# Out-state weights of an S5 layer on three engines: power 0 to ScalarE, input products to VectorE, one-input forms for the smallest VectorE operations

## The chip, the core and the metric

The kernel runs on one core of a Trainium2 chip as one program. The metric is device time in microseconds. Five engines run their own in-order instruction queues and wait for one another through semaphores: TensorE (PE, matmul), VectorE (DVE), ScalarE (ACT), GpSimd (POOL) and SyncE (SP), which here issues nearly all DMAs.

## The reference

Two post-norm layers share one residual stream of 512 latent and 256 context tokens, 1024 wide. Layer 0 is windowed grouped-query attention, layer 1 a bidirectional diagonal state space (S5). Cut to what matters:

```python
for i in range(2):
    h = x * (1 + scale) + shift; hc = xc * (1 + scale_c) + shift_c
    pz = h @ w_in; pzc = hc @ w_in          # p: mixer input, z: gate path
    y, yc = attention_mixer(...) if i == 0 else s5_mixer(...)
    x = layer_norm(alpha * x + gate * ((y * silu(z)) @ w_out), g, b)
    if i == 0:                              # the same for xc
        xc = layer_norm(alpha * xc + gate_c * ((yc * silu(zc)) @ w_out), g, b)

def softmax_with_sink(s, sink):             # one more logit per head
    return softmax(concat([s, sink]))[..., :-1]

def s5_scan(u, abar, bbar, cmat, h0):       # per 128-token chunk, 2 directions
    bu = einsum('btgn,gpn->btgp', u, bbar)  # complex states, 64 per group
    hs = associative_scan(a * h + bu)
    y = einsum('btgp,gnp->btgn', hs, cmat).real
```

abar, bbar and cmat depend on parameters alone. The kernel computes from them, while layer 0 runs, the weights with which layer 1 works on blocks of tokens.

## The kernel before

**The weights.** Layer 1 needs 64 in-state weights (`gen_w`) and 32 out-state weights (`gen_o`, numbered q = 0 to 31). One out-state weight is two halves `gO` of 128 x 576: 4 groups by 9 powers (0 to 8) of the transition by 16 channels. Each half is a real and an imaginary product and their sum: L931 (`gO` = `gcb` x powers), L932 (`gX`, the same with the other part), L933 (`gO` = `gO` + `gX`). Before them three small operations make the input coefficients: L919 and L920 (two products of 128 x 128, into the two halves of a `gX` tile) and L921 (`gbb`, 128 x 256, their sum). All run on POOL, except for q = 3, 7 and 11, which run on DVE as a whole. `gX` has one buffer for both engines, `gO` four (three in the second pool), `gcb`, `gpp` and `gbb` two each.

**What follows a weight.** SP writes the halves to DRAM (`osc`, L936). A closure `lag` then multiplies `gbb` with `gO` on PE (L948, 16 short matmuls), ACT and DVE copy the result to `gK` (L954 to L957), and SP writes it to `ksc` (L958); every eighth weight also starts eight DMAs that reorder it (`m0sc`, L974). The lag of one weight is issued behind the products of the next. PE works through its queue in order, so a lag whose weight is late holds up all matmuls behind it.

**Where the weights are made.** Layer 0 calls `bg(n)` between its steps; behind the in-state weights it opens a pool `go` (`open_o`, four `gO` buffers) and asks for out-state weights 0 to QA - 1 = 26. The output projection of layer 0 (`outproj0`) calls `side()` between token blocks; the first NB = 3 calls make the other five from a pool `go2` with three `gO` buffers. A scheduler with priorities sets each engine's order; a weight's products are given a priority of GP = 80 ahead of their place, a lag LP = 50.

**Attention.** `att_s` takes two heads at a time: scores on PE (`S`), mask and negated maximum on DVE (L445, L453, and L454 on context tokens, 128 x 2), exponentials on ACT (L461, L463), the row sum plus sink (L464, 128 x 2) and its reciprocal on DVE, the scaling on ACT (L467). `att_o` transposes on PE (`PT`), splits into a high and a low half on ACT and DVE (`pth`, `ptl`) and multiplies with the values.

**The norm and layer 1's input.** `norm` takes statistics on DVE and an inverse root by an integer guess and three Newton steps of two operations each on 128 x 1 (L293, L294); `nrm` (L631) normalizes 128 x 512. `make_h1` transposes the rows on PE (`h1t`), applies scale and shift on 128 x 128 pieces, four on DVE (L1018) and four on ACT (L1020) of each eight, and splits the result into `H1H` (ACT) and `H1L` (DVE). In `outproj0` PE multiplies the gated attention (`gr`, split to `gh` and `gl`) with `wout` (split to `woh` and `wol`) into `po`.

Every fp32 matmul operand goes through such a split and every product is three matmuls (L155 to L157).

## Time and profile before

| | us |
|---|---|
| median of 3 runs (1504.64 to 1512.83) | 1510.47 |
| the profiled execution | 1508.56 |
| its span in the trace | 1506.8 |
| PE busy | 1404.2 (93%) |
| DVE busy | 1040.2 (69%) |
| ACT busy | 645.8 (43%) |
| POOL busy | 635.0 (42%) |

The mean granted clock of PE was 0.971 of full speed. Each engine's busy time is the sum over its instructions; the share is of the span. An engine that is busy for less than the span was either not needed or waiting, and which of the two it was is read stage by stage. Stages in the trace: layer 0 up to about 655 us (the last in-state weight leaves POOL at 468.25 us and out-state weights follow), `outproj0` from there to about 870 us, then layer 1.

### The profile page before, as it was taken

What the parts mean: (1) busy time and instruction counts of PE and PEld (TensorE: products, weight loads), DVE (VectorE), ACT (ScalarE), POOL (GpSimd) and SP (SyncE); (2) the same over time, 40 slices, a digit from 0 to 9 for tenths busy, and PEclk for the clock granted to TensorE, in tenths of its full rate; (3) what the DMA queues carried; (4) which work ended last, traced back from release to release, by engine and by line L of the source; (5) the groups of instructions that cost most, each with busy time, mean ns of one, the idle gap of its engine ahead of it and who ended that gap; (6) DMA issues with size and microseconds to landing.
All of it is one profiled execution on the core that took longest, in us unless ns stands there. A gap on an engine that the chain in (4) does not pass through costs nothing.

```text
span 1506.8 us, 25662 instructions
## 1 busy us (share of the span) xinstructions
PE 1404.2 (93%) x9092; PEld 1134.5 (75%) x9092; DVE 1040.2 (69%) x2711; ACT 645.8 (43%) x1256; POOL 635.0 (42%) x542
## 2 busy tenths in 40 slices
PE   7999999999997899987988799999999999999997
PEld 2554789988886788875766688888777777888886
DVE  7734748777684477876759922789887896565376
ACT  1310546555464446552333234445556545343220
POOL 0004469999998676988975800000000000000240
PEclk9999999999998899998999899999999999999999
DMA  9876566766664446488795476667666796655541
GB/s 335 274 232 203 163 192 202 225 214 208 200 221 152 131 146 200 141 248 265 214 280 158 137 257 226 210 210 231 220 226 220 223 292 213 197 195 168 180 152 60
DMA packets 252639, 309.57 MB, mean 205 GB/s; under 512 B 45408, under 2 KB 151648, under 8 KB 252512
## 3 DMA queue, kind: packets, MB, share of 16 engines
q1 hardware_dynamic: 227168, 295.36, 61.5%
q10 hardware_dynamic: 25344, 12.59, 2.9%
q8 instruction: 71, 1.16, 0.3%
q14 instruction: 56, 0.46, 0.1%
HBM read 239.20 MB, written 77.07 MB: 210 GB/s over the span
## 4 chain that ended last, share of the span: by engine, by line
PE 54%; POOL 13%; DVE 13%; DMA 10%; issue 5%; ACT 3%; SPq 1%; POOLq 0%; DVEq 0%; ACTq 0%
PE pg L155 4%; PE pg L157 4%; PE pg L156 4%; PE adaps L166 3%; PE po L156 3%; PE po L157 3%; PE po L155 3%; DMA wsc<-gW 3%; PE ins L1084 3%; POOL gm L885 3%; POOL gm L886 2%; PE pul L155 2%; PE pul L156 2%; PE pul L157 2%; POOL gW L888 2%
## 5 line engine op out<-in xcount | busy, mean ns | idle before, releaser
L1318 POOL TENSOR_TENSOR xt<-xt,lng 128x512 f32<-128x512 f32 (+1 forms) x9 | 13.7, 1532 | 584.5 <-DMA xt<-n0sc 584.5
L146 DVE TENSOR_TENSOR wl<-wr,wh 128x1024 fp32r<-128x1024 f32 x104 | 137.8, 1325 | 142.9 <-ACT wh L145 140.3
L145 ACT ACTIVATE wh<-wr 128x1024 fp32r<-128x1024 f32 x104 | 109.9, 1057 | 188.0 <-PE pc L156 52.0
L155 PE MATMUL pg<-ga,wh 128*128 128x512 f32 x256 | 100.3, 392 | 0.8 <-ACT ga L1243 0.8
L157 PE MATMUL pg<-ga,wl 128*128 128x512 f32 x256 | 100.5, 393 | 0.0
L933 POOL TENSOR_TENSOR gO<-gO,gX 128x576 f32<-128x576 f32 x58 | 94.9, 1635 | 4.4
L885 POOL TENSOR_TENSOR gm<-gB,gE 128x512 f32<-128x512 f32 x56 | 78.6, 1403 | 23.6 <-DVE zs L500 19.3
L931 POOL TENSOR_TENSOR gO<-gcb,gpp 128x576 f32<-128x576 f32 x58 | 77.0, 1333 | 25.2 <-PE lag L948 20.6
L932 POOL TENSOR_TENSOR gX<-gcb,gpp 128x576 f32<-128x576 f32 x58 | 82.1, 1415 | 2.8
L886 POOL TENSOR_TENSOR gm<-gB,gE 128x512 f32<-128x512 f32 x56 | 82.6, 1475 | 0.0
L461 ACT ACTIVATE P<-P,nm 128x512 f32<-128x512 f32 (+1 forms) x64 | 49.7, 776 | 76.3 <-DVE nm L445 76.2
L487 DVE TENSOR_TENSOR ptl<-PT,pth 128x512 fp32r<-128x512 f32 (+1 forms) x96 | 60.9, 639 | 22.6 <-ACT pth L486 21.9
L1107 DVE TENSOR_TENSOR x<-m 128x64 f32<-128x64 f32 x376 | 74.7, 217 | 2.4
L146 DVE TENSOR_TENSOR gl<-gr,gh 128x512 fp32r<-128x512 f32 x48 | 50.2, 1047 | 31.2 <-ACT gh L145 31.2
L467 ACT ACTIVATE P<-P,es 128x512 f32<-128x512 f32 (+2 forms) x96 | 60.5, 682 | 19.7 <-DVE es L465 19.6
L155 PE MATMUL pq<-hh,wh 128*128 128x512 f32 x160 | 66.0, 413 | 2.8 <-ACT hh L255 2.8
L486 ACT ACTIVATE pth<-PT 128x512 fp32r<-128x512 f32 (+1 forms) x96 | 52.4, 559 | 34.4 <-PE PT L483 26.0
L483 PE MATMUL PT<-ident,P 128*128 128x128 f32 x352 | 61.3, 282 | 6.2 <-DVE vl L388 2.8
L155 PE MATMUL po<-woh,gh 128*128 128x512 f32 (+1 forms) x156 | 59.9, 394 | 7.5 <-ACT woh L580 4.7
L156 PE MATMUL pq<-hl,wh 128*128 128x512 f32 x160 | 65.8, 412 | 0.8 <-DVE hl L256 0.8
L157 PE MATMUL pq<-hh,wl 128*128 128x512 f32 x160 | 64.9, 406 | 0.3 <-DVE wl L146 0.3
L156 PE MATMUL po<-wol,gh 128*128 128x512 f32 (+1 forms) x156 | 61.7, 395 | 3.5 <-DVE wol L581 3.5
(317 smaller groups left out, 4673.2 us busy)
## 6 DMA issues: line engine op xcount, KB each, us to landing
wr<-w SPq DMA_DIRECT2D x40, 512.0 KB
osc<-gO SPq DMA_DIRECT2D x64, 256.0 KB
wr<-wout SPq DMA_DIRECT2D x32, 512.0 KB
W<-wsc SPq DMA_DIRECT2D x32, 512.0 KB
om<-osc SPq DMA_DIRECT2D x64, 256.0 KB
wr<-glu SPq DMA_DIRECT2D x32, 512.0 KB
gE<-esc SPq DMA_DIRECT2D x56, 256.0 KB
gB<-bt SPq DMA_DIRECT2D x56, 256.0 KB
```

Of the source, the lines that this page charges most:

```text
L145: nc.scalar.activation(hi, raw, AF.Copy)
L146: nc.vector.tensor_sub(lo, raw, f32(hi))
L155: mm(out, wh, mh, start=start, stop=False)
L156: mm(out, wh, ml, start=False, stop=False)
L157: mm(out, wl, mh, start=False, stop=stop)
L483: nc.tensor.transpose(T[:, j, h, :], P[h][:, c * 128:(c + 1) * 128], k.ident)
L885: tt(x(m1), x(B), eb(0), op=ALU.mult)
L886: tt(x(m2), x(B), eb(1), op=ALU.mult)
L931: eng.tensor_tensor(o, cc(0), pb(0), op=ALU.mult)
L932: eng.tensor_tensor(x, cc(1), pb(36), op=ALU.mult)
L933: last = eng.tensor_tensor(o, o, x, op=ALU.add)
L1107: nc.vector.tensor_add(x, m[:, :, 0], m[:, :, 1])
```

## The change

Seven edits. In `norm`, L454 and L464 the operation with two inputs from SBUF becomes `tensor_scalar`, which takes the second input as a per-partition scalar; L454 and L464 become two operations of 128 x 1 for one of 128 x 2. In `gen_o` the products of the input coefficients and their sum (L919 to L921) go to DVE for every q and get a tile `gby` of their own; the column of power 0 is a copy of `gcb` with a sign, done by ACT (`sg`, loaded in `open_o`), so that L931 to L933 take 8 powers for 9 (128 x 512 for 128 x 576). In `make_h1` all eight pieces go to ACT. QA, NB becomes 20, 5: layer 0 makes 20 weights, and `outproj0` 12 over five calls.

```diff
--- before.py
+++ after.py
@@ -290,8 +290,8 @@
         nt = pool.tile([128, 6], F32, name="nt")
         for i in range(3):
             t, yn = nt[:, 2 * i:2 * i + 1], nt[:, 2 * i + 1:2 * i + 2]
-            nc.vector.scalar_tensor_tensor(t, y, xe[:, i:i + 1], y, op0=ALU.mult, op1=ALU.mult)
-            nc.vector.scalar_tensor_tensor(yn, t, -3.0, y, op0=ALU.add, op1=ALU.mult)
+            nc.vector.tensor_scalar(t, y, xe[:, i:i + 1], y, op0=ALU.mult, op1=ALU.mult)
+            nc.vector.tensor_scalar(yn, t, -3.0, y, op0=ALU.add, op1=ALU.mult)
             y = yn
         return mv[:, 0:1], y
 
@@ -448,10 +448,11 @@
         Sc = k.ps.tile([128, 2, 256], F32, name="S", tag="S", bufs=2)
         for h in range(2):
             scores(h, Sc[:, h], C, 384, nw)
-        hs = slice(2 * p, 2 * p + 2)
         if not lat:
             nc.vector.tensor_reduce(mc, Sc, axis=AX.X, op=ALU.max)
-            nc.vector.scalar_tensor_tensor(nm, mc, -SCALE, k.nsink[:, hs], op0=ALU.mult, op1=ALU.min)
+            for h in range(2):
+                nc.vector.tensor_scalar(nm[:, h:h + 1], mc[:, h:h + 1], -SCALE, k.nsink[:, 2 * p + h:2 * p + h + 1],
+                                        op0=ALU.mult, op1=ALU.min)
         for h in range(2 if lat else 0):
             Sw = k.ps.tile([128, 512], F32, name="S", tag="S", bufs=2)[:, :nw]
             scores(h, Sw, slice(kb0 * 128, kb1 * 128), 128 if qb == 0 else 0, 0)
@@ -461,7 +462,8 @@
             nc.scalar.activation(P[h][:, :n], src, AF.Exp, bias=nm[:, h:h + 1], scale=-1.0 if lat else SCALE, accum_out=sm[:, h:h + 1])
         for h in range(2):
             nc.scalar.activation(es[:, h:h + 1], nm[:, h:h + 1], AF.Exp, bias=k.sink[:, 2 * p + h:2 * p + h + 1])
-        nc.vector.tensor_add(es, es, sm)
+        for h in range(2):
+            nc.vector.tensor_scalar(es[:, h:h + 1], es[:, h:h + 1], sm[:, h:h + 1], None, op0=ALU.add)
         nc.vector.reciprocal(es, es)
         for h in range(2):
             nc.scalar.activation(P[h][:, :n], P[h][:, :n], AF.Copy, scale=es[:, h:h + 1])
@@ -894,6 +896,9 @@
     k.gob, k.dq = gob, q0
     k.dd = pool.tile([128, 16 * (q1 - q0)], F32, name="dd")
     k.nc.sync.dma_start(k.dd, k.a["dd"][:, 16 * q0:16 * q1])
+    sg = pool.tile([128, 2], F32, name="sg")
+    k.nc.sync.dma_start(sg, k.a["sgn"])
+    k.sg = sg[:, 0:1]
 
 
 def gen_o(k, pool, q):
@@ -908,7 +913,7 @@
     dd = k.dd
     O = []
     bb = pool.tile([128, 8, 2, 16], F32, name="gbb", bufs=2)
-    t = pool.tile([128, 4, 9, 16], F32, name="gX", bufs=1).rearrange("p g k n -> p (g k n)")
+    t = pool.tile([128, 256], F32, name="gby")
     by, bx = (t[:, 128 * i:128 * i + 128].rearrange("p (d g n) -> p d g n", d=2, g=4) for i in range(2))
 
     def qb(o):
@@ -916,21 +921,24 @@
 
     def dup(t):
         return t.rearrange("p d g n -> p (d g) n")[:, :, None].to_broadcast([128, 8, 2, 16])
-    eng.tensor_tensor(by, cb[:, 2], qb(72), op=ALU.mult)
-    eng.tensor_tensor(bx, cb[:, 3], qb(76), op=ALU.mult)
-    eng.tensor_tensor(bb, dup(by), dup(bx), op=ALU.add)
+    nc.vector.tensor_tensor(by, cb[:, 2], qb(72), op=ALU.mult)
+    nc.vector.tensor_tensor(bx, cb[:, 3], qb(76), op=ALU.mult)
+    nc.vector.tensor_tensor(bb, dup(by), dup(bx), op=ALU.add)
     for d in range(2):
         o = pool.tile([128, 4, 9, 16], F32, name="gO", bufs=k.gob)
         x = pool.tile([128, 4, 9, 16], F32, name="gX", bufs=1)
 
         def cc(t):
-            return cb[:, t, d][:, :, None].to_broadcast([128, 4, 9, 16])
+            return cb[:, t, d][:, :, None].to_broadcast([128, 4, 8, 16])
 
         def pb(o_):
-            return pp[:, d, o_:o_ + 36].rearrange("p (g k) -> p g k", g=4)[:, :, :, None].to_broadcast([128, 4, 9, 16])
-        eng.tensor_tensor(o, cc(0), pb(0), op=ALU.mult)
-        eng.tensor_tensor(x, cc(1), pb(36), op=ALU.mult)
-        last = eng.tensor_tensor(o, o, x, op=ALU.add)
+            return pp[:, d, o_:o_ + 36].rearrange("p (g k) -> p g k", g=4)[:, :, 1 - d:9 - d][:, :, :, None].to_broadcast([128, 4, 8, 16])
+
+        nc.scalar.activation(o[:, :, 8 * d], cb[:, 0, d], AF.Copy, scale=k.sg)
+        o8, x8 = o[:, :, 1 - d:9 - d], x[:, :, 0:8]
+        eng.tensor_tensor(o8, cc(0), pb(0), op=ALU.mult)
+        eng.tensor_tensor(x8, cc(1), pb(36), op=ALU.mult)
+        last = eng.tensor_tensor(o8, o8, x8, op=ALU.add)
         O.append(o)
         x0 = 1 - d
         nc.sync.dma_start(k.osc[q, :, :, :, d].rearrange("p u r x -> p (u r) x"),
@@ -1014,10 +1022,7 @@
         for i in range(4):
             kk = 4 * j + i
             g, c = k.h1g[:, r, kk:kk + 1], k.h1b[:, r, kk:kk + 1]
-            if j == 0:
-                nc.vector.tensor_scalar(hf[:, kk], t[:, i], g, c, op0=ALU.mult, op1=ALU.add)
-            else:
-                nc.scalar.activation(hf[:, kk], t[:, i], AF.Identity, bias=c, scale=g)
+            nc.scalar.activation(hf[:, kk], t[:, i], AF.Identity, bias=c, scale=g)
     H, Lo = k.H1[r]
     ts = slice((b - 4 * r) * 128, (b - 4 * r) * 128 + 128)
     nc.scalar.activation(H[:, :, ts], hf, AF.Copy)
@@ -1332,7 +1337,7 @@
 
 N0, NW, EW = 1, 22, 8
 QO, QN = 32, 1
-QA, NB = 27, 3
+QA, NB = 20, 5
 PP = 300
 GP = 80
 XP = 100
```

The first weight on DVE, where the order has left the in-state weights behind (`zt`, `zs`: gate path; `P`, `nm`: scores of attention; `ptl`: the low half of the transposed scores). Before:

```order
L403 SCALAR_TENSOR_TENSOR zt<-zt,pzl 128x512
L445 ISA P,mx<-S,mask,nsink 128x256
L445 ISA mx 128x1
L404 TENSOR_TENSOR zs<-zt,zs 128x512
L445 ISA P,nm<-S,mask,mx 128x256
L445 ISA nm 128x1
L487 TENSOR_TENSOR ptl<-PT,pth 128x512
```

After:

```order
L403 SCALAR_TENSOR_TENSOR zt<-zt,pzl 128x512
L445 ISA P,mx<-S,mask,nsink 128x256
L445 ISA mx 128x1
L404 TENSOR_TENSOR zs<-zt,zs 128x512
L924 TENSOR_TENSOR gby<-gcb,gpp 128x128
L925 TENSOR_TENSOR gby<-gcb,gpp 128x128
L445 ISA P,nm<-S,mask,mx 128x256
L445 ISA nm 128x1
L489 TENSOR_TENSOR ptl<-PT,pth 128x512
L926 TENSOR_TENSOR gbb<-gby 128x256
```

The three operations of weight 0 now stand in DVE's queue ahead of scores and transposed scores.

The same place on POOL, from the last product of the in-state weights. Before:

```order
L888 TENSOR_TENSOR gW<-gm_4537,gm_4538 128x4x64
L919 TENSOR_TENSOR gX<-gcb,gpp 128x128
L920 TENSOR_TENSOR gX<-gcb,gpp 128x128
L931 TENSOR_TENSOR gO<-gcb,gpp 128x576 x2
L921 TENSOR_TENSOR gbb<-gX 128x256
L931 TENSOR_TENSOR gO<-gcb,gpp 128x576 x2
L932 TENSOR_TENSOR gX<-gcb,gpp 128x576
L933 TENSOR_TENSOR gO<-gO,gX 128x576
L932 TENSOR_TENSOR gX<-gcb,gpp 128x576
L933 TENSOR_TENSOR gO<-gO,gX 128x576
```

After:

```order
L890 TENSOR_TENSOR gW<-gm_4565,gm_4566 128x4x64
L939 TENSOR_TENSOR gO<-gcb,gpp 128x4x128
L940 TENSOR_TENSOR gX<-gcb,gpp 128x4x128
L939 TENSOR_TENSOR gO<-gcb,gpp 128x4x128 x3
L941 TENSOR_TENSOR gO<-gO,gX 128x4x128
L940 TENSOR_TENSOR gX<-gcb,gpp 128x4x128
L941 TENSOR_TENSOR gO<-gO,gX 128x4x128
```

Eleven operations stood on POOL up to the second sum of weight 0, and eight stand there now, none of them with `gX` as the input coefficients' tile.

A weight in the midst of attention on DVE, where the lag of weight 4 is copied out (L956 and L957 before, L964 and L965 after). Before:

```order
L361 TENSOR_TENSOR qf<-t 64x512 x2
L956 TENSOR_TENSOR gK<-lag,dd 128x16
L957 TENSOR_TENSOR gK<-lag,gK 128x16
L487 TENSOR_TENSOR ptl<-PT,pth 128x512
L146 TENSOR_TENSOR wl<-wr,wh 128x1024
```

After:

```order
L926 TENSOR_TENSOR gbb<-gby 128x256
L489 TENSOR_TENSOR ptl<-PT,pth 128x512
L924 TENSOR_TENSOR gby<-gcb,gpp 128x128
L925 TENSOR_TENSOR gby<-gcb,gpp 128x128
L964 TENSOR_TENSOR gK<-lag,dd 128x16
L965 TENSOR_TENSOR gK<-lag,gK 128x16
L466 TENSOR_SCALAR es<-es,sm 128x1
L489 TENSOR_TENSOR ptl<-PT,pth 128x256
```

The products of weight 7 now stand ahead of the copy of weight 4's lag, and behind them the sums and the splits of the scores.

The end of `outproj0` on DVE, where the first norms meet the first pieces of layer 1's input (`R`: residual rows; `st`, `mv`, `xe`, `ih`, `nt`: steps of the norm). Before:

```order
L282 BN_AGGR mv<-st 128x2
L1018 TENSOR_SCALAR h1f<-h1t,h1g,h1b 128x128 x4
L285 SCALAR_TENSOR_TENSOR xe<-mv,nscale 128x3
L280 BN_STATS st<-R_8848 128x6
L287 TENSOR_SCALAR ih<-xe 128x1
L625 TENSOR_TENSOR R_9662<-po,gate_8451 128x512
L288 TENSOR_SCALAR ih<-ih 128x1
L146 TENSOR_TENSOR gl<-gr,gh 128x512
L626 SCALAR_TENSOR_TENSOR R_9662<-xt,R_9662 128x512
L293 SCALAR_TENSOR_TENSOR nt<-ih,xe 128x1
```

After:

```order
L280 BN_STATS st<-R_9794 128x6
L287 TENSOR_SCALAR ih<-xe 128x1
L146 TENSOR_TENSOR gl<-gr,gh 128x512
L1029 TENSOR_TENSOR H1L_8279<-h1f,H1H_8278 128x8x128
L282 BN_AGGR mv<-st 128x2
L288 TENSOR_SCALAR ih<-ih 128x1
L146 TENSOR_TENSOR gl<-gr,gh 128x512
L285 SCALAR_TENSOR_TENSOR xe<-mv,nscale 128x3
L293 TENSOR_SCALAR nt<-ih,xe 128x1
```

The pieces of layer 1's input are gone from this queue, and the Newton steps have the one-input form. On PE the lags stand closer together in `outproj0`: 98 `po` matmuls between one lag and the second one after it before, about 66 now, and the last lag stands 97 `po` matmuls ahead of the last one, where before it stood behind it.

## Rows read from the trace of the kernel before

**Rows 1.** The page: engines (busy us, share of span, instructions), and the chain.

```profile
PE 1404.2 (93%) x9092; PEld 1134.5 (75%) x9092; DVE 1040.2 (69%) x2711; ACT 645.8 (43%) x1256; POOL 635.0 (42%) x542
...
PE 54%; POOL 13%; DVE 13%; DMA 10%; issue 5%; ACT 3%; SPq 1%; POOLq 0%; DVEq 0%; ACTq 0%
```

**Rows 2.** Stretches: us, busy (x) of PE, PEld, DVE, ACT, POOL; clock, DMA.

```profile
470.00:530.00 60.00, 44.64 (x307) 37.98 (x306) 27.63 (x73) 26.05 (x67) 40.82 (x41) 0.86 0.47 146
530.00:650.00 120.00, 118.18 (x907) 104.69 (x906) 94.30 (x203) 71.87 (x188) 96.05 (x84) 1.00 0.54 163
650.00:710.00 60.00, 46.76 (x265) 35.69 (x264) 41.76 (x50) 21.36 (x44) 53.09 (x43) 0.89 0.89 270
710.00:780.00 70.00, 68.75 (x378) 54.24 (x376) 51.41 (x53) 23.31 (x39) 67.78 (x51) 1.00 0.82 241
780.00:806.00 26.00, 20.60 (x97) 15.36 (x87) 14.80 (x45) 6.29 (x13) 2.07 (x2) 0.87 0.75 235
806.00:870.00 64.00, 47.05 (x331) 40.36 (x333) 62.62 (x112) 20.36 (x44) 55.57 (x45) 0.87 0.41 131
```

**Rows 3.** Timeline, POOL: start, us, operation, count [idle before, releaser].

```profile
474.41 0.40 POOL L919 TENSOR_TENSOR gX<-gcb,gpp 128x128 f32<-128x128 f32 x1 [5.42 <-DMA gpp<-ppsc]
```

**Rows 4.** Timeline, PE: the first lag.

```profile
486.87 1.08 PE L948 MATMUL lag<-gO,gbb 128*32 128x128 f32 x16 [8.74 <-POOL gO L933]
```

**Rows 5.** Waits of PE, 450 to 900 us: total us, times, longest.

```profile
PE h1t L1013 <- DVE nrm L631: 13.8, 5, 5.8
...
PE lag L948 <- POOL gO L933: 9.9, 3, 8.7
...
PE S L155 <- DVE nm L445: 5.8, 1, 5.8
```

**Rows 6.** The chain of waits, 640 to 712 us: start, us, what.

```profile
667.53 2.29 POOL gO L931 x2
...
671.02 4.02 DMA ksc<-gK
...
675.06 6.28 DMA wr<-wout
```

**Rows 7.** POOL by line, 710 to 780 us: busy us, mean ns.

```profile
L933 POOL TENSOR_TENSOR gO<-gO,gX 128x576 f32<-128x576 f32 x12 | 21.2, 1766 | 0.9
L932 POOL TENSOR_TENSOR gX<-gcb,gpp 128x576 f32<-128x576 f32 x12 | 19.2, 1603 | 0.5
L931 POOL TENSOR_TENSOR gO<-gcb,gpp 128x576 f32<-128x576 f32 x11 | 15.6, 1422 | 0.4 <-PE lag L948 0.4
```

**Rows 8.** DVE by line, 806 to 870 us.

```profile
L1018 DVE TENSOR_SCALAR h1f<-h1t,h1g,h1b 128x128 f32<-128x128 f32 x24 | 8.2, 396 | 0.0
...
L293 DVE SCALAR_TENSOR_TENSOR nt<-nt,xe 128x1 f32<-128x1 f32 x8 | 5.5, 688 | 0.1
...
L294 DVE SCALAR_TENSOR_TENSOR nt<-nt 128x1 f32<-128x1 f32 x8 | 4.1, 510 | 0.1
...
L293 DVE SCALAR_TENSOR_TENSOR nt<-ih,xe 128x1 f32<-128x1 f32 x4 | 3.1, 764 | 0.1
...
L294 DVE SCALAR_TENSOR_TENSOR nt<-nt,ih 128x1 f32<-128x1 f32 x4 | 2.4, 598 | 0.0
...
L287 DVE TENSOR_SCALAR ih<-xe 128x1 int32<-128x1 int32 x4 | 0.6, 141 | 0.0
```

**Rows 9.** Waits of DVE, 450 to 900 us.

```profile
DVE gX L919 <- POOL gO L933: 8.2, 2, 6.3
```

**Rows 10.** The tile gX on DVE: min/median/max ns, first and last start.

```profile
L919 DVE TENSOR_TENSOR gX<-gcb,gpp x3: 281/293/293, 503.4 to 589.5; 128x128 f32<-128x128 f32 x3
```

**Rows 11.** The tile h1f on ACT.

```profile
L1020 ACT ACTIVATE h1f<-h1t,h1b,h1g x24: 448/458/467, 810.9 to 869.8; 128x128 f32<-128x128 f32 x24
```

## The prediction

> **What bounds the kernel now.** I read first the page's engine line and chain of waits: PE is busy for 1404.2 of 1506.8 us, and the chain runs 54% through PE, 13% each through POOL and DVE and 10% through DMAs [rows 1]. So about 100 us of PE's idle time is all that can be had, and only where something that the change touches ends the wait. The busy time by stretch says where that is [rows 2]. From 530 to 650 us PE is busy 118.18 of 120 us, from 710 to 780 us 68.75 of 70: nothing is to be won there. Idle are 15.4 us from 470 to 530, 13.2 from 650 to 710, 5.4 from 780 to 806 and 17.0 from 806 to 870, 51 us together, with the granted clock at 0.86 to 0.89 in each (its mean falls below full speed just where PE idles). The four have different limits: POOL's first out-state weight, the start of `outproj0` behind a backlog, and twice DVE, which is busy for 62.62 of the 64 us up to 870.
>
> **First weight, 470 to 530 us.** POOL starts when `gpp` has landed, at 474.41 [rows 3], and lag 0 runs on PE at 486.87, after a wait of 8.74 us [rows 4]: eleven POOL operations in 12.5 us. Eight are left, all sums and products of half weights shortened by 1/9. What goes is the three small ones, 0.40 us for L919 [rows 3], the same for L920 and twice that for L921 by its size, 1.6 us together, and 1/9 of the rest, 1.2 us. Lag 0 can run at about 484. But it now stands some 5 us of PE work earlier in PE's queue, and the three coefficient operations and ACT's power-0 columns now wait for the same `gcb` ahead of attention's work. At an equal place of PE's work this is 484 + 1.1 + 5 = 490 for 488: a loss of 2. Against it stands the next dip: DVE waited 6.3 us for POOL's sum because both use the one `gX` buffer [rows 9], and PE 5.8 us for DVE's `nm` [rows 5]; the coefficients no longer take `gX`, but the products of q = 3 still do. I take 0, between a loss of 6 (the gap longer, the dip kept) and a gain of 6 (the dip gone).
>
> **Attention, 530 to 650 us.** PE has 1.8 us of idle time, so fewer weights on POOL, shorter ones and the lighter L454 and L464 are worth nothing here. DVE gets three operations for each weight that was POOL's: two like L919's 0.29 us [rows 10] and one of twice the size, about 1 us if they run alone. ACT gets two small copies, each below the 0.458 us of a 128x128 piece [rows 11]. DVE is busy 94.30 and ACT 71.87 of 120 us [rows 2], so PE's work hides both; uncovered it would be up to 2 us a weight. From +2 to -5; I take 0.
>
> **Start of outproj0, 650 to 710 us.** Here POOL's products of attention's last weights still run, 53.09 of 60 us [rows 2], and the chain goes from POOL's products through `ksc` (4.02 us) and a load of `wout` (6.28 us) [rows 6], because SP, in order, holds the load behind a weight's `osc` and `ksc`. With weights 20 to 31 moved behind, weight 19 is the last of its pool and POOL has seven weights fewer up to here; at 11.7 us each (below) the backlog is gone. What is late next is the load of `wout` itself, with DMAs busy 0.89 of the time [rows 2]. Of the 13.2 us idle I take 9; bounds 0 (the load was the limit all along) and 15 (all of it, and the clock).
>
> **First half of outproj0, 710 to 780 us.** PE is full, POOL too (67.78 of 70 us). Twelve half-weight sums [rows 7], so six weights, in 70 us make 11.7 us a weight; PE does 49 `po` matmuls and a lag of 1.08 us [rows 4] in that time, 0.217 us a matmul. The new order has 33 matmuls between lags: 33 x 0.217 + 1.08 = 8.2 us a weight. POOL needs 2 x (1.766 + 1.603 + 1.422) x 8/9 = 8.5 us [rows 7]. Over 11 gaps POOL falls 3 us behind, and I charge 3. It has three buffers, so it can be a weight and a half ahead, some 13 us, at the start: that is the lower bound, 0. The upper one is POOL's old pace, the second rival.
>
> The coefficient operations read two SBUF tiles on DVE beside POOL, as most stretched rows do: a 128x1 Newton step with two inputs takes 510 to 764 ns, a one-input step beside it 141 [rows 8]. The Trainium skill (SBUF — State Buffer, section Who interferes with whom) states that a VectorE operation with two SBUF inputs contends with a GpSimd operation that reads SBUF, which speaks against moving these three. Going by that difference, up to 0.6 us, they would cost 1.8 us more a weight, 22 us of DVE over twelve; DVE has 18.6 free in these 70 us alone [rows 2], so the sum stays.
>
> **Norms and layer 1's input, 780 to 870 us.** PE waits 13.8 us for `nrm` [rows 5], and DVE is the limit. Off DVE go the Newton steps' stretch, 5.5 + 4.1 + 3.1 + 2.4 = 15.1 us for 24 operations that at the one-input 0.141 us take 3.4 [rows 8]: 11.7 us. The pieces `h1f` go too, 8.2 us [rows 8]; ACT pays 24 x 0.458 = 11 us [rows 11] on 20.36 of 64, which leaves it half free. DVE gains one to two weights' coefficients in this stretch, 1 to 4 us. That is 16 to 19 us off a full DVE. Moreover the last lag moves 97 `po` matmuls (21 us) ahead of the end, so POOL is quiet for most of the norms and stretches less of what stays. What is late next is PE itself, 47.05 of 64 us busy at clock 0.87, so the 17.0 idle us and some clock are the ceiling there, and the wait from 780 to 806 for a load of `gr` may stay. I take 20; bounds 0 (ACT or `gr` takes DVE's place) and 28.
>
> **Sum.** 0 + 0 + 9 - 3 + 20 = 26 us off the profiled execution's 1508.56: 1482.5. That execution lies 1.9 us under the median of 1510.47, well within the 0.5% (7.5 us) which is about what a measurement of this kernel can tell from no change. Layer 1 is untouched but for the last norm, where POOL is quiet: nothing. The forecast's own range is 1470 to 1500.
>
> **Rivals.**
> - *All dips close.* With DVE and POOL out of the way, only the first weight's gap of some 9 us is left of the 51: 1508.6 - 42, and a little clock: 1465. For it: every one of the four stretches has a releaser that the change touches. Against: DMAs at 0.75 to 0.89 in two of them [rows 2]. Chance 0.13.
> - *POOL keeps its pace in outproj0.* If DVE's traffic, not the nine operations, sets 11.7 us a weight, the denser lags hold PE for 11 x (11.7 - 8.2) = 38 us less the head start of 13: 25 lost in place of 3, 1482.5 + 22 = 1504, no change. For it: POOL at 97% there. Against: 1/9 and three operations do go. Chance 0.14.
> - *Slower: in-order waits in attention.* Twenty weights, in place of three, now have operations in DVE's queue that wait for `gcb`, whose buffer POOL frees only when it has done the weight two before; in the new order weight 7's stand ahead of the copy of lag 4 and the splits of the scores behind it. Of the three weights on DVE two had such a wait, 8.2 us in all [rows 9], 2.7 us a weight, and PE's wait was 5.8 us [rows 5], 0.7 of it. Twenty times 2.7 x 0.7 is 38 us: 1520. It decides from 26 / (20 x 0.7) = 1.9 us a weight, and shows as slower from 2.4. Against: both waits were for `gX`, which is no longer shared, and POOL has fewer operations. Chance 0.11.
> - *The one-input forms wait too.* Then the Newton steps keep their stretch, 11.7 us stay, and the time is 1494. For it: `nrm`, a one-input form of 128x512, is the operation that PE waits for [rows 5]. Against: the 141 ns of the 128x1 form beside POOL [rows 8]. Chance 0.07. [...]
>
> **How the numbers follow.** The forecast has 0.55. Faster by over 0.5% is its 0.55, 0.13, 0.07 and none of the others: 0.75. No change is the pace: 0.14. Slower is the in-order wait: 0.11. The range leaves out slower's 0.11 and a little below: 1459 to 1510; nearly all the chance lies on one side.
>
> **What would show it.** Right: PE's wait for `nrm` under 4 us, Newton steps near 0.15 us, no `h1f` on DVE, PE busy over 90% where 46.76 of 60 us were, POOL near 8.5 us a weight in `outproj0`. Wrong: DVE idle before `gby` behind a DMA, ACT idle before the power-0 copy, with PE waiting for `nm` or `pth` in attention; lags of `outproj0` waiting for POOL's sum more than 0.5 us each; or Newton steps still at 0.5 us and more.

## The result and the profile after

The changed kernel takes 1518.83 us (median of 20 runs, 1509.80 to 1525.03) for 1507.26 of the kernel before in as many: the ratio is 1.0073, with a 95% interval of 1.0055 to 1.0091. It is slower by 0.7%; 1482.5 had been forecast, 1459 to 1510 was the range, and slower had 0.11.

The page's engine line and chain after, which answer to [rows 1]:

```profile
PE 1407.7 (93%) x9092; PEld 1130.1 (75%) x9092; DVE 1073.1 (71%) x2838; ACT 667.3 (44%) x1344; POOL 549.4 (36%) x455
...
PE 54%; DVE 16%; DMA 11%; POOL 8%; issue 5%; ACT 4%; SPq 2%; POOLq 0%; ACTq 0%; DVEq 0%
```

DVE's work grew by 33 us and its share of the chain from 13 to 16%; POOL's work fell by 86 us, and its share from 13 to 8%. Three of the five points that POOL lost in the chain came back as DVE's, the others mostly as DMA's and ACT's.

The same stretches as in [rows 2], in the same columns:

```profile
470.00:530.00 60.00, 42.56 (x276) 36.33 (x277) 40.69 (x93) 28.13 (x77) 34.54 (x30) 0.80 0.46 146
530.00:650.00 120.00, 113.23 (x843) 96.73 (x842) 103.13 (x224) 69.60 (x192) 77.25 (x59) 1.00 0.53 160
650.00:710.00 60.00, 56.70 (x366) 45.68 (x364) 39.50 (x89) 30.75 (x79) 22.08 (x17) 0.97 0.71 204
710.00:780.00 70.00, 63.15 (x296) 47.64 (x297) 52.66 (x62) 21.08 (x41) 41.64 (x30) 0.93 0.69 206
780.00:806.00 26.00, 20.85 (x123) 15.88 (x122) 21.25 (x25) 10.03 (x21) 21.51 (x15) 0.93 1.02 315
806.00:870.00 64.00, 52.27 (x323) 41.33 (x322) 62.62 (x121) 27.20 (x67) 38.27 (x29) 0.95 0.64 196
```

From 530 to 650 us, where PE had been busy for 118.18 of 120 us, it is now busy for 113.23; from 710 to 780, where it had been full, for 63.15 of 70. But the stretches no longer hold the same work. To compare, I take the starts of the same PE matmuls in both traces: the 241st transpose of attention (`PT`), the first, 101st and 451st `po`, the first `pul` of layer 1, and the last `po` of the kernel. The table has the length of each stage before, in us, and by how much it is longer or shorter after and in the runs that are told of below (one profiled execution each; these lie up to 5.4 us off the medians that are given below, so a few us in one cell prove nothing):

| stage | before | after | e1 | e4 | e5 | e7 | e8 | e12 | e13 | e14 | e15 | e16 | e17 |
|---|---|---|---|---|---|---|---|---|---|---|---|---|---|
| to transpose 241 | 518.9 | +15.4 | +3.6 | +1.4 | -1.5 | +2.8 | +6.5 | +1.1 | +2.5 | +0.9 | +1.2 | +15.6 | +0.3 |
| rest of attention | 150.1 | +8.5 | -1.2 | -4.9 | +15.8 | -1.7 | -4.0 | -5.1 | +18.5 | +2.4 | -2.1 | +7.4 | +17.6 |
| outproj0, 100 po | 37.0 | -8.7 | -12.4 | +6.1 | -12.9 | -11.7 | +0.3 | -1.6 | -11.1 | -8.3 | -5.9 | -13.3 | -11.6 |
| to po 451 | 96.7 | +19.2 | +11.4 | +4.2 | +15.2 | +23.1 | +4.3 | -2.0 | +18.0 | +6.2 | -0.2 | +26.1 | +13.3 |
| to layer 1 | 67.9 | -20.0 | -9.8 | +0.3 | -13.2 | -19.3 | +5.4 | -5.9 | -18.1 | -10.1 | -6.8 | -22.8 | -18.4 |
| rest | 626.4 | -4.7 | -5.2 | -3.6 | -4.6 | +0.7 | +1.8 | -1.2 | -1.0 | -4.4 | -3.8 | -2.2 | +1.2 |

The start of `outproj0` won 8.7 us (9 had been said) and the norms 20.0 (20 had been said). The loss stands in three stages that had been put at 0, 0 and 3: the first weight, attention's body, and the first half of `outproj0`. Together the stages up to `outproj0` lost 23.9 us, for 0 forecast, and the three of `outproj0` won 9.5, for 26 forecast; 4.7 were won in layer 1, where nothing had been forecast.

**The first weight.** DVE's timeline (start, us, operation, and in brackets the idle time before it and its releaser):

```profile
462.75 0.97 DVE L404 TENSOR_TENSOR zs<-zt,zs 128x512 f32<-128x512 f32 x1
476.95 1.16 DVE L924 TENSOR_TENSOR gby<-gcb,gpp 128x128 f32<-128x128 f32 x1 [13.24 <-DMA gcb<-cb]
```

ACT's and POOL's at the same place:

```profile
476.72 0.81 ACT L937 ACTIVATE gO<-gcb,sg 128x64 f32<-128x64 f32 x2 [14.41 <-issue]
```

```profile
471.72 0.72 POOL L890 TENSOR_TENSOR gW<-gm,gm 128x256 f32<-128x256 f32 x1
476.91 1.06 POOL L939 TENSOR_TENSOR gO<-gcb,gpp 128x512 f32<-128x512 f32 x1 [4.46 <-DMA gpp<-ppsc]
```

And what PE waited for from 435 to 535 us:

```profile
PE S L155 <- DVE nm L445: 14.1, 2, 12.7
PE PT L485 <- DVE vl L388: 4.3, 1, 4.3
...
PE S L155 <- DVE mx L445: 1.5, 1, 1.5
```

DVE comes to the first coefficient product at 463.7 us and stands still for 13.24 us, since `gcb` is loaded only when POOL has left the in-state weights, at 472.4, and their pool is free. ACT stands still for 14.41 us at its first power-0 copy. The operations of the first scores stand behind both, and PE waits up to 12.7 us for `nm`. Before, these operations were POOL's, and POOL had nothing else to do [rows 3]; PE's waits were 8.74 us, for the lag [rows 4], and 5.8 for `nm` [rows 5].

**Attention.** DVE's waits from 450 to 900 us, and the three operations in the whole trace (min/median/max ns), with their sum from 540 to 690 us:

```profile
DVE gby L924 <- DMA gcb<-cb: 13.2, 1, 13.2
...
DVE gbb L926 <- PE lag L956: 11.3, 5, 5.9
DVE gby L924 <- DMA gpp<-ppsc: 11.3, 3, 4.4
```

```profile
L924 DVE TENSOR_TENSOR gby<-gcb,gpp x32: 267/876/1346, 477.0 to 837.0; 128x128 f32<-128x128 f32 x32
L925 DVE TENSOR_TENSOR gby<-gcb,gpp x32: 272/282/1368, 478.0 to 837.2; 128x128 f32<-128x128 f32 x32
L926 DVE TENSOR_TENSOR gbb<-gby x32: 414/1224/1527, 480.1 to 843.0; 128x256 f32<-128x256 f32 x32
```

```profile
540.00:690.00 150.00, 26.00 (x37) 1.00 0.57 168
```

Two waits of [rows 9] have become nine: for `gcb`, for `gpp`, and, five times, of `gbb` for PE's lag (it has two buffers, and a new one may only be written when the lag of the weight two before has read its own). The operations cost 26.00 us of DVE for some 12 weights, 2.1 us a weight; 1 had been said.

**Start and first half of outproj0.** The first 100 `po` matmuls and the 350 behind them, of the kernel before:

```profile
669.00:706.00 37.00, 28.64 (x135) 21.44 (x134) 23.72 (x21) 9.13 (x15) 34.51 (x28) 0.86 0.91 284
706.00:802.70 96.70, 90.05 (x479) 69.80 (x478) 65.77 (x92) 30.99 (x56) 71.00 (x52) 0.96 0.79 236
```

The same after, and PE's waits there after (692 to 837 us):

```profile
692.90:721.20 28.30, 24.84 (x105) 19.60 (x102) 13.19 (x17) 7.89 (x14) 0.00 (x0) 0.94 0.85 259
721.20:837.10 115.90, 96.19 (x496) 72.02 (x495) 97.76 (x121) 34.73 (x75) 90.87 (x64) 0.94 0.77 232
```

```profile
PE po L157 <- DVE gl L146: 10.5, 5, 4.8
PE lag L956 <- DVE gK L965: 5.4, 3, 3.5
PE po L155 <- DVE R L627: 3.5, 1, 3.5
```

In the first half DVE does 97.76 us of work where it had done 65.77, and PE waits for DVE's `gl`, `gK` and `R`. POOL's pace is the one that was forecast: 90.87 us for 64 operations, six to a weight, are 8.5 us a weight. That POOL starts ahead was wrong:

```profile
685.89 1.46 POOL L941 TENSOR_TENSOR gO<-gO,gX 128x512 f32<-128x512 f32 x1
723.10 1.29 POOL L939 TENSOR_TENSOR gO<-gcb,gpp 128x512 f32<-128x512 f32 x1 [35.76 <-PE po L156]
```

Between weight 19 and weight 20 POOL stands idle for 35.76 us, so the twelve weights fall on the end of the stage.

**The norms.** Newton's steps in the whole trace of the kernel before and of the one after (min/median/max ns):

```profile
L293 DVE SCALAR_TENSOR_TENSOR nt<-nt,xe x20: 210/219/1208, 802.2 to 1501.8; 128x1 f32<-128x1 f32 x20
L294 DVE SCALAR_TENSOR_TENSOR nt<-nt x20: 136/159/1116, 802.5 to 1502.1; 128x1 f32<-128x1 f32 x20
```

```profile
L293 DVE TENSOR_SCALAR nt<-nt,xe x20: 258/272/274, 837.5 to 1511.7; 128x1 f32<-128x1 f32 x20
L294 DVE TENSOR_SCALAR nt<-nt x20: 199/210/217, 837.8 to 1512.0; 128x1 f32<-128x1 f32 x20
```

The longest of PE's waits that is left in this stage:

```profile
PE pul L155 <- ACT h1f L1025: 2.2, 1, 2.2
```

After, they take 272 and 210 ns and at most 274 and 217, for means of 510 to 764 in this stage before; PE's 13.8 us for `nrm` [rows 5] are gone. They do not take the 141 ns of the integer steps, on which the forecast rested. With a median of 219 and 159 ns the two-input form was the shorter one wherever it was not stretched, so the one-input form costs some 50 ns a step there.

### The profile page after: what moved, and what is told of

It reads as the page before. It is cut to its first block, busy times and chain, and to the rows that moved or that the text cites. A ratio compares the mean times of both kernels' runs of the same rounds, so it can differ in the third digit from the quotient of the medians.

```text
span 1516.6 us, 25857 instructions
## 1 busy us (share of the span) xinstructions
PE 1407.7 (93%) x9092; PEld 1130.1 (75%) x9092; DVE 1073.1 (71%) x2838; ACT 667.3 (44%) x1344; POOL 549.4 (36%) x455
## 4 chain that ended last, share of the span: by engine, by line
PE 54%; DVE 16%; DMA 11%; POOL 8%; issue 5%; ACT 4%; SPq 2%; POOLq 0%; ACTq 0%; DVEq 0%
PE pg L157 4%; PE pg L155 4%; PE pg L156 4%; PE adaps L166 3%; DMA wsc<-gW 3%; PE ins L1089 3%; PE po L157 3%; PE po L155 3%; PE po L156 3%; PE pul L155 2%; ACT X L1132 2%; PE pul L156 2%; PE pul L157 2%; DVE wl L146 2%; PE pq L156 2%
## 5 line engine op out<-in xcount | busy, mean ns | idle before, releaser
L146 DVE TENSOR_TENSOR wl<-wr,wh 128x1024 fp32r<-128x1024 f32 x104 | 141.2, 1358 | 140.0 <-ACT wh L145 139.2
L939 POOL TENSOR_TENSOR gO<-gcb,gpp 128x512 f32<-128x512 f32 x58 | 70.6, 1233 | 108.6 <-PE po L156 35.8
L941 POOL TENSOR_TENSOR gO<-gO,gX 128x512 f32<-128x512 f32 x58 | 89.0, 1535 | 3.0
L940 POOL TENSOR_TENSOR gX<-gcb,gpp 128x512 f32<-128x512 f32 x58 | 74.9, 1291 | 38.4 <-PE PT L485 13.2
L157 PE MATMUL po<-woh,gl 128*128 128x512 f32 (+1 forms) x156 | 60.8, 391 | 10.1 <-DVE gl L146 10.1
L155 PE MATMUL S<-kh,qh 128*128 128x256 f32 (+1 forms) x160 | 50.9, 320 | 20.1 <-DVE nm L445 17.0
```

Source lines behind the costliest of these rows:

```text
L146: nc.vector.tensor_sub(lo, raw, f32(hi))
L155: mm(out, wh, mh, start=start, stop=False)
L157: mm(out, wl, mh, start=False, stop=stop)
L939: eng.tensor_tensor(o8, cc(0), pb(0), op=ALU.mult)
L940: eng.tensor_tensor(x8, cc(1), pb(36), op=ALU.mult)
L941: last = eng.tensor_tensor(o8, o8, x8, op=ALU.add)
```

## The experiments

Each was timed in five rounds against the kernel before on the same chip.

| run | median us | ratio to before | 95% interval |
|---|---|---|---|
| after | 1518.8 | 1.0073 | 1.0055 to 1.0091 |
| e1 coefficients on POOL | 1493.8 | 0.9899 | 0.9878 to 0.9920 |
| e2 power 0 in the products | 1529.8 | 1.0151 | 1.0123 to 1.0180 |
| e3 both undone | 1500.1 | 0.9944 | 0.9926 to 0.9963 |
| e4 before + one-input forms | 1513.6 | 1.0041 | 1.0025 to 1.0057 |
| e5 coefficients late | 1513.0 | 1.0025 | 1.0007 to 1.0042 |
| e6 e1, power 0 late | 1493.6 | 0.9907 | 0.9881 to 0.9934 |
| e7 coefficients on DVE in outproj0 only | 1498.3 | 0.9927 | 0.9905 to 0.9949 |
| e8 before + 20 and 12 weights | 1519.4 | 1.0055 | 1.0032 to 1.0077 |
| e9 all products on POOL | 1515.4 | 1.0043 | 1.0027 to 1.0060 |
| e10 e1, h1f split | 1496.5 | 0.9912 | 0.9888 to 0.9936 |
| e11 e1, nm and es two-input | 1492.5 | 0.9896 | 0.9873 to 0.9918 |
| e12 e1, 27 and 5 weights | 1494.3 | 0.9915 | 0.9887 to 0.9943 |
| e13 first three on POOL | 1520.2 | 1.0093 | 1.0062 to 1.0125 |
| e14 extra load without waits | 1500.1 | 0.9944 | 0.9921 to 0.9968 |
| e15 three edits alone | 1494.3 | 0.9921 | 0.9891 to 0.9951 |
| e16 lags whole | 1520.4 | 1.0074 | 1.0051 to 1.0098 |
| e17 e13, lags whole | 1515.9 | 1.0046 | 1.0025 to 1.0067 |
| e18 e1, lags whole | 1497.8 | 0.9910 | 0.9882 to 0.9938 |

**e1, which edit.** In the changed kernel:

```diff
-    nc.vector.tensor_tensor(by, cb[:, 2], qb(72), op=ALU.mult)
+    eng.tensor_tensor(by, cb[:, 2], qb(72), op=ALU.mult)
...
```

(the same for `bx` and `bb`).

> The changed kernel with one edit undone: the three operations on the input coefficients run again on the engine of the weight's products (POOL, and DVE for q = 3, 7, 11), in the tile gby. Theory A (DVE's in-order queue waits for gcb and gpp ahead of attention's work: 13.2, 11.3 and 11.3 us of DVE waits in the changed kernel, PE waiting 12.7 us for nm behind the first of them): the first weight costs attention some 10 us less, and the whole kernel is 15 to 25 us faster than the changed one, 1494 to 1504. Theory B (it is ACT's power-0 copies that hold up ACT's queue, 14.4 us at the first weight): little changes, 1514 to 1520. Theory C (more weights in outproj0 is what costs): 1514 to 1520.

Measured 1493.8: the coefficients on DVE cost 25 us, and without them the change is a gain of 1.0%. Theory A names the edit rightly. ACT's copies still hold up the start, and PE waits longer than it did for `nm` in the changed kernel (12.7 us):

```profile
PE O L155 <- ACT zs L499: 16.1, 1, 16.1
```

but by the end of attention little of it is left in the stages: +3.6 and -1.2 us. So the stop of PE at the first weight is not in itself what the 25 us are.

**e2 and e3.** Power 0 back in the products, alone and with e1's edit:

```diff
-        nc.scalar.activation(o[:, :, 8 * d], cb[:, 0, d], AF.Copy, scale=k.sg)
-        o8, x8 = o[:, :, 1 - d:9 - d], x[:, :, 0:8]
+        o8, x8 = o, x
...
```

> The changed kernel with one edit undone: power 0 is computed again in the 128x576 products, and ACT copies none. Theory A (DVE's wait): ACT's 14.4 us wait at the first weight goes, but DVE's 13.2 stays and PE waits as before; POOL's products are 1/8 longer; 1516 to 1526. Theory B (ACT's wait): 10 to 20 us faster than the changed kernel, 1499 to 1509. Theory C: 1516 to 1526.

> Both undone: the weights are made as before, in 9 powers and with the coefficients on their own engine; left of the change are the one-input forms, h1f on ACT and 20 + 12 weights. Theory A: 1494 to 1506, like the run with the coefficients alone undone, a little over it since POOL's products are longer. Theory B: 1496 to 1506. Theory C (20 + 12 costs in outproj0, where POOL at 11.7 us a weight would hold PE): 1515 and more.

1529.8 and 1500.1. Theory B falls, and with e3 theory C; 1529.8 is 4 us above A's range as well. Power 0 on ACT, with its eight-power products, wins 6 us (e1 against e3) to 11 (after against e2).

**e4.** The one-input forms in the kernel before, as the change has them:

```diff
-            nc.vector.scalar_tensor_tensor(nm, mc, -SCALE, k.nsink[:, hs], op0=ALU.mult, op1=ALU.min)
+            for h in range(2):
+                nc.vector.tensor_scalar(nm[:, h:h + 1], mc[:, h:h + 1], -SCALE, ...)
...
```

> The kernel before with the one-input forms alone (norm, nm, es). The prediction's term: 11.7 us off DVE in the stretch of the norms, at least half of it on PE's wait for nrm: 1496 to 1504, Newton steps near 0.15 us. The rival (they wait for GpSimd too): 1506 to 1510, Newton steps at 0.5 us and more.

1513.6, neither of the two: slower by 0.4%, though the Newton steps take 272 ns and attention's body is 4.9 us shorter. The norms win nothing (+0.3), and the two stages ahead of them lose 6.1 and 4.2. PE's waits from 690 to 800 us and a piece of the chain of waits show where: the load of `wout`, which SP issues behind POOL's last weights, begins at 691.16 and lands at 697.8. In the kernel before, this load was issued at 684.61, 6.6 us earlier; why POOL's weights are later here is not shown.

```profile
PE po L155 <- ACT woh L583: 11.3, 1, 11.3
```

```profile
691.16 6.66 DMA wr<-wout
697.84 1.07 ACT woh L583
```

**e5 and e6, is it the place in the queue?** The three operations (e5) and, with e1's edit, ACT's copies (e6) ordered behind the weight's last sum:

```diff
+    for i_ in (nc.vector.tensor_tensor(by, ...), nc.vector.tensor_tensor(bx, ...), nc.vector.tensor_tensor(bb, ...)):
+        k.tc.add_manual_dep(ins_of(i_), ins_of(last).name, ...NoSync...)
...
```

> The changed kernel with the three coefficient operations still on DVE for all 32 weights, but ordered behind the weight's last sum: the same work on DVE beside the same work on POOL, only later in DVE's queue, when gcb has long landed. Theory A1 (the in-order wait at the head of DVE's queue is what costs): the waits gby<-gcb and gby<-gpp go, and the time comes near that of the coefficients on POOL, 1494 to 1503. Theory A2 (DVE's load and its contention with POOL cost, wherever the operations stand): 1512 to 1520.

> The coefficients on POOL, and ACT's power-0 copies ordered behind the half's sum: what is left of the in-order wait, on ACT (PE waited 16.1 us for zs behind the first copies), is taken away. If the in-order wait on ACT still costs: 1485 to 1491, 3 to 8 us faster than with the coefficients on POOL alone (1493.8). If PE makes up for it later in attention anyhow: 1492 to 1496.

e5: all of DVE's waits before `gby` and `gbb` are gone and the first stage costs nothing (-1.5, of which some 2 are nine `pq` matmuls that moved into the next stage), though PE still waits 9.5 us there for ACT's `zs`. But attention's body costs 15.8 in place of 8.5, and PE now waits for the late sums in `outproj0`:

```profile
PE lag L958 <- DVE gbb L945: 14.5, 5, 5.6
```

1513.0: 6 us won, A2's figure; the rows under e16 show that it need not be A2's cause. e6 changed nothing (1493.6), as its second expectation had it, though PE's longest wait at the first weight fell from 16.1 to 6.1 us.

**e7, where.** For the three operations:

```diff
+    ce = eng if q < QA else nc.vector
```

> The coefficients on DVE only for the 12 weights of outproj0, on POOL for attention's 20. Theory A1 (waits in attention's DVE queue): most of the 25 us between the changed kernel and the one with the coefficients on POOL comes back: 1493 to 1500. Theory A3 (the coefficients cost in outproj0, where PE waited 10.5 us for gl and DVE is full): 1508 to 1519.

1498.3: of the 25 us, 20.5 are attention's weights. The first half of `outproj0` is no shorter than in the changed kernel (+23.1), but the norms behind it give most of that back (-19.3).

**e8.** In the kernel before:

```diff
-QA, NB = 27, 3
+QA, NB = 20, 5
```

> The kernel before with 20 weights in layer 0 and 12 over five calls of outproj0 alone. The prediction's terms: start of outproj0 9 us won, the first half 3 or more lost; with nine-power weights of 11.7 us on POOL against lags 33 matmuls apart the loss is the larger. If POOL's pace holds PE (the second rival): 1515 to 1530. If not: 1498 to 1506.

1519.4, slower by 0.55%, in the range of the second rival: nothing won at the start of `outproj0` (+0.3), 4.3 lost in its first half, where PE waits for POOL's sums (the longest 3.2 us), and 5.4 behind (the 6.5 of the first stage are not explained, and this profiled execution is 4.3 us over the median):

```profile
PE lag L948 <- POOL gO L933: 7.2, 3, 3.2
```

**e9.** In the changed kernel:

```diff
-    eng = nc.vector if q % n == n - 1 else nc.gpsimd
+    eng = nc.gpsimd
```

> The changed kernel with the products of the weights q = 3, 7 and 11 on POOL too (DVE does only the coefficients): 18 operations of 0.68 us, 12 us, off DVE during attention, while POOL there is busy only 77 of 120 us. Theory A2 (DVE's load in attention costs, besides the wait at the first weight): 6 to 12 us faster than the changed kernel, 1507 to 1513. Theory A1 (only the waits for gcb and gpp cost): 1515 to 1521, or slower, since three more weights come from POOL.

1515.4: 3.4 us better than the changed kernel with overlapping intervals, at the lower edge of A1's range. It speaks against A2 and settles nothing, since POOL now makes three more weights.

**e10 to e12, what the other edits are worth in e1.** `h1f` split again (e10); `nm` and `es` as before (e11); the coefficients' tile `gX` again and 27 and 5 weights (e12):

```diff
+            if j == 0:
+                nc.vector.tensor_scalar(hf[:, kk], t[:, i], g, c, op0=ALU.mult, op1=ALU.add)
...
+        nc.vector.tensor_add(es, es, sm)
...
+QA, NB = 27, 3
```

> The kernel with the coefficients on POOL (1493.8), with h1f split between DVE and ACT as before. The prediction's term: h1f takes 8.2 us off a full DVE at the end of outproj0: 1498 to 1503. The rival (ACT pays 11 us for it, and the last h1f of each block is later): 1490 to 1494.

> The kernel with the coefficients on POOL, with nm and es in their two-input forms of 128x2 again and only the norm's Newton steps changed. Prediction's term: nothing in attention, 1492 to 1496. If the doubled count costs attention: 1488 to 1492. If the one-input forms are worth it: 1496 to 1500.

> The kernel with the coefficients on POOL (in the tile gX as before, which makes it fit), with 27 weights in layer 0 and 5 in outproj0 as before. The prediction's terms: start of outproj0 9 us, and POOL quiet in the norms some 9 of the 20: 1503 to 1512 without them. The rival (12 lags 33 matmuls apart cost in the first half of outproj0 what the rest wins, as 20 + 12 alone made the kernel before slower): 1485 to 1494.

1496.5, 1492.5 and 1494.3: all three lie within e1's interval or overlap it. None of these edits is worth anything measurable there; e10 lies between its two ranges, so it does not decide what `h1f` is worth. With 20 and 12 weights the gain at the start of `outproj0` and in the norms (-12.4, -9.8) is paid in its first half (+11.4); with 27 and 5 there is less of each (-1.6, -5.9, -2.0).

**e13 and e14, wait or load?** `ce = eng if q < 3 else nc.vector` in the changed kernel (e13). In e1, with the coefficients in the tile `gX` again, three extra DVE operations for each of attention's weights on a constant tile (e14), which compute nothing that is used:

```diff
+    if q < QA:
+        w = pool.tile([128, 256], F32, name="load", bufs=1)
+        for i_ in (nc.vector.tensor_tensor(w[:, 0:128], k.ident, k.ident, op=ALU.mult),
+                   nc.vector.tensor_tensor(w[:, 128:256], k.ident, k.ident, op=ALU.mult),
+                   nc.vector.tensor_tensor(w, w, w, op=ALU.add)):
...
```

> The changed kernel with the coefficients of weights 0, 1 and 2 alone back on POOL; 29 weights' coefficients stay on DVE. If the wait at the head of DVE's queue at the first weight is worth what the stage shows (some 12 of the 25 us between the changed kernel and the one with all coefficients on POOL): 1505 to 1510. If that wait is made up for later and the load in attention's body decides: 1514 to 1520.

> The kernel with the coefficients on POOL (in gX), and for each of attention's 20 weights three extra DVE operations of the same forms (two of 128x128, one of 128x256, all inputs in SBUF) on a constant tile, ordered behind the weight's last sum: no engine waits for them and they wait for no load. If the load on DVE in attention costs in itself: 1500 to 1508, 6 to 14 us over 1493.8, the loss spread over 540 to 690 us. If only waits cost: 1492 to 1497.

e13 took DVE's first wait away, and the first stage lost 2.5 us in place of 15.4. PE still stands still at the first weight, now behind ACT's copies:

```profile
PE O L155 <- ACT zs L499: 12.0, 1, 12.0
```

The time stayed, 1520.2: the body of attention costs 18.5 us in place of 8.5, and DVE still waits there:

```profile
DVE gby L925 <- DMA gpp<-ppsc: 6.3, 4, 4.4
...
DVE gbb L927 <- PE lag L957: 4.1, 3, 2.5
```

e14 costs 6 us (1500.1), the lower end of what the load was to cost; in its profiled execution attention is 3.3 us longer than before. Its operations take 22.70 us from 540 to 690 us, 1.6 us a weight, and DVE is busy there for 125.29 us, as in the changed kernel (124.60). So neither DVE's first wait nor the load explains 20 us.

**e15.** Power 0 on ACT, one-input Newton steps and `h1f` on ACT, and nothing else, in the kernel before.

> The kernel before with three of the edits alone: power 0 on ACT, one-input Newton steps in the norm, h1f on ACT (coefficients on POOL in gX, 27 and 5 weights, nm and es as before). If the other four edits are worth nothing or cost: 1488 to 1495. If 20 + 12 weights and the one-input nm and es belong to the gain: 1496 to 1503.

1494.3: this smallest version has the whole gain; its interval overlaps those of e1 and e11.

**e16 to e18, split lags.** In the changed kernel's trace a lag stands in pieces between other matmuls:

```profile
655.22 0.41 PE L956 MATMUL lag<-gO,gbb 128*32 128x128 f32 x2
655.55 0.49 PE L155 MATMUL pzl<-hh,wh 128*128 128x512 f32 x1
655.98 0.41 PE L956 MATMUL lag<-gO,gbb 128*32 128x128 f32 x2
656.31 0.49 PE L156 MATMUL pzl<-hl,wh 128*128 128x512 f32 x1
```

A piece and a large matmul take 0.76 us together, where a large one alone takes some 0.24 and a whole lag of 16 small ones, as here in e16, 0.64:

```profile
656.30 0.64 PE L957 MATMUL lag<-gO,gbb 128*32 128x128 f32 x16
```

They were put together again in the changed kernel, in e13 and in e1:

```diff
+        with k.tc.high_priority(offset=200):
             for d in (1, 0):
                 for g in range(4):
...
```

> The changed kernel with a higher priority for the lag's matmuls alone: in PE's order each of the 32 lags stands in one piece again, where the changed kernel has 53 pieces (the kernel before 32, the one with the coefficients on POOL 39, coefficients late 65, first three on POOL 51, the extra load alone 37). In the traces a whole lag takes 0.57 us, a piece of two matmuls 0.34, and the large matmuls beside it step at 0.42 in place of 0.24. Theory S (the split lags are the loss in attention's body): 6 to 10 us faster than the changed kernel, 1508 to 1513; the first weight's wait stays. Theory A2 (DVE's load itself): 1515 to 1521.

> The same priority in the kernel with the first three weights' coefficients on POOL (1520.2, 51 pieces), so that the first wait and the split lags are both gone while 29 weights' coefficients stay on DVE. Theory S: the two causes together, 1497 to 1506. Theory A2: 1512 to 1520.

> The same priority in the kernel with all coefficients on POOL (1493.8, 39 pieces, all of the split ones at the start of outproj0): a control for what the priority does by itself. 1490 to 1495 if it is neutral but for those pieces; 1496 and more if the earlier place makes PE wait for POOL's sums.

1520.4, 1515.9 and 1497.8. The control, e18, is not clear of e1 (their intervals overlap), but lies in its second range, and PE waits there for POOL's sums (12.2 us from 690 to 800 us, 8.3 in e1). Theory S falls for the changed kernel: the pieces are gone, and attention is as long as before (+15.6 and +7.4). With DVE's first wait gone too (e17) some 4 us are won, with overlapping intervals; PE still waits 9.9 us for ACT's `zs` there.

What became of the time shows in attention's body, from transpose 241 to the first `po`, in the columns of [rows 2]. After, e1, e14, e5 and e16:

```profile
534.30:692.90 158.60, 150.50 (x1119) 126.77 (x1117) 132.36 (x293) 95.57 (x259) 95.18 (x73) 0.99 0.57 169
522.50:671.40 148.90, 143.23 (x1104) 125.25 (x1102) 108.21 (x256) 94.57 (x256) 117.34 (x112) 0.98 0.61 184
519.90:672.30 152.40, 145.31 (x1102) 126.27 (x1101) 130.56 (x302) 94.66 (x258) 121.54 (x112) 0.98 0.59 176
517.40:683.30 165.90, 158.70 (x1116) 130.55 (x1115) 132.59 (x295) 98.18 (x263) 93.27 (x73) 0.98 0.57 170
534.50:692.00 157.50, 144.06 (x1120) 124.14 (x1118) 130.38 (x293) 94.51 (x261) 92.93 (x73) 1.00 0.59 175
```

In the changed kernel PE idles for 8.1 us and is busy for 7.3 more than in e1, on nearly the same matmuls: mostly the pieces. In e16 the pieces are gone and PE is busy for 144.06 us, but it idles for 13.4. In e5, with the most pieces (65 runs of lag matmuls in PE's order, for 53 after and 39 in e1), PE idles for no more than 7.2 us, and the loss is PE's own time, 158.70 for 143.23 us, some 2 of it for the nine `pq` matmuls. By these rows the pieces and the waits hide one another in the changed kernel, and what e5 lost is not shown to be DVE's load. A run with both gone, e5 with whole lags, was not made.

## Why the prediction was wrong

- **First weight, "I take 0".** This is the step that failed first. It counted POOL's chain up to lag 0 and charged PE's later place. It named that the coefficient operations and ACT's copies wait ahead of attention's work, but not from when: from DVE's own arrival at 463.7 us, nine us before POOL has left the old pool. 15.4 us were lost at this stage, 11.8 more than in e1. The stop of PE there is not the difference (12.7 us, 16.1 in e1, 12.0 in e13); by these rows it is what follows on DVE, which waits again for `gpp` (4.4 us) and for PE's lag (5.9), while PE waits for DVE's `vl`, `mx` and `nm` (4.3, 1.5 and 1.4 us; none over 0.7 in e1).
- **Attention, "PE's work hides both".** Priced at 1 us of DVE a weight, measured 2.1; the forecast had named that price as an estimate beside POOL (1.8 us more), but only for `outproj0`. And the cover was the wrong measure. That PE is full says that it waits for nothing now, not that DVE can be late: DVE was busy for 79% of the stretch from 530 to 650 us and is now for 86%, with operations in its queue that wait for loads and for PE's lag. Nor did the forecast ask what late `gbb` do to PE's own order, where lags now stand in pieces. e7 puts attention's share of the 25 us at 20.5.
- **The slower rival** had the sign, the place and nearly the time (1520), with a chance of 0.11. Its mechanism is only partly shown: the waits at the head of DVE's queue are there (13.2, 11.3 and 11.3 us in all, 36 where it had 54), but taking all of them away (e5) won 6 us and taking the first away (e13) nothing. That the time came out near is thus in part luck. What is left by elimination is the chain that now runs through two in-order queues for each weight, DVE's coefficients for PE's lag and PE's lag for DVE's next `gbb`, together with the lags in pieces. No run took both away and left the work, so it is not shown; a third `gbb` buffer was not tried.
- **Start of outproj0, 9.** Right in size (8.7), by luck, and wrong in its reason: 20 and 12 weights alone gave nothing there (e8); lighter weights and the fewer of them together give it (e1 -12.4; e15, with 27 and 5, -5.9).
- **First half of outproj0, -3.** Measured -19.2. POOL's pace was looked at, and came out at 8.5 us a weight as forecast; DVE's was not; and POOL had no head start. But no run got faster by mending it: what is lost there comes back in the norms. The sum of the three stages of `outproj0`, put at 26 won, lies between 7.9 and 12.9 in e1, e7, e12, e13, e15 and after.
- **Norms, 20.** Measured 20.0, and the agreement is luck. The reason given was DVE's lighter work, with Newton steps at 141 ns; they take 272 and 210. The same steps and the same `h1f` win 9.8 in e1, where PE still waits 8.5 us for `nrm`, 6.8 in e15 and 5.9 in e12, and the one-input forms alone win nothing in this stage (e4, +0.3). In the table the stage is shortest in after, e7 and e16, whose first half of `outproj0` was longest. That the one-input form is not stretched held; the rival that it waits too is out.
- **Parts add up only in the right company.** 20 and 12 weights alone +11 us, one-input forms alone +6; those two with `h1f` on ACT -8 (e3); power 0 a further 6 off (e1); coefficients on DVE +25.

## What to carry to other kernels

An operation moved to a busy engine's queue costs what stands behind it, counted from when that engine gets there and not from when the data are ready; read the new order for what follows it, and the trace for when the engine arrives. Ask too what the later result does to the order of the engine that uses it: when one loss is mended, the other may show in its place (e16, e5). Being off POOL is no gain where POOL has time: here the cheapest version keeps the coefficients on POOL, with power 0 on ACT, Newton steps with a per-partition scalar and `h1f` on ACT, and takes 0.992 of the time (0.989 to 0.995). A gain in front of a load can be given back at that load, if it is issued no earlier (in e4 it was issued later).

## What the runs showed of the hardware

- A Newton step of 128x1 with two tensor inputs took 510 to 764 ns in the mean in the stretch where POOL worked beside it, with medians of 219 (L293) and 159 ns (L294) of 20 executions each over the whole kernel; with the second input as a per-partition scalar it took 258 to 274 (L293) or 196 to 217 ns (L294) in all 30 executions of each, whether POOL worked or not. The Trainium skill (SBUF — State Buffer, section Who interferes with whom) states that a VectorE operation with at most one SBUF input, outside the two-port modes, does not contend with GpSimd, and that one with two contends with a GpSimd operation that reads SBUF; these numbers agree with both halves.
- A coefficient product of 128x128 with two SBUF inputs on DVE took 267 to 1368 ns, its median 876 for the first of each pair and 282 for the second.
- Two small lag matmuls (128x32 weights) between 128x512 ones cost 0.76 us with one large one, which alone takes 0.24, so a lag in eight pieces costs some 4 us for the 0.64 of a whole one; yet whole lags gave no time back in e16.
